# Four-head gated linear attention: own-tile products placed right behind each head's state products, gates traced later, the first two heads' sums in other PSUM banks

## The chip, the cores and the metric

The kernel runs on one core of a Trainium2 chip. The metric is the device time of one execution in microseconds (us). The engines of the core work side by side: TensorE (PE in the profile, its weight loads PEld), VectorE (DVE), ScalarE (ACT), GpSimd (POOL) and SyncE (SP, which here only starts transfers). Each engine works through its own instructions in order and waits where one needs another engine's result.

## The reference: what is computed

A trunk of two layers on 512 tokens of width 1024: layer 0 mixes with multi-head latent attention, layer 1 with gated linear attention (GLA), and each mixer is followed by a squared-ReLU MLP; a last RMS norm closes. The change touches the GLA mixer alone. Its four heads have keys of 128 and values of 256 columns. With `b_` the running sum of the log gates, the reference does per chunk of tokens:

```python
def step(state, inp):
    q_, k_, v_, b_ = inp
    o_inter = jnp.einsum('bhcd,bhde->bhce', q_ * jnp.exp(b_), state)
    ...
    attn = jnp.einsum('bhtd,bhsd,bhtsd->bhts', q_, k_, decay)
    o_intra = jnp.einsum('bhts,bhse->bhte', attn, v_)
    ...
    new_state = (state * jnp.exp(b_last[:, :, 0, :, None])
                 + jnp.einsum('bhsd,bhse->bhde', k_ * jnp.exp(b_last - b_), v_))
    return new_state, o_inter + o_intra
...
o = rms_norm(o, g_norm)
o = o * jax.nn.silu(g.astype(jnp.float32)).reshape(B, S, GLA_HEADS, GLA_HEAD_V)
return o.reshape(B, S, GLA_DV).astype(xn.dtype) @ w_o
```

The output of a head is thus a part from the tokens of its own chunk (`o_intra`) and a part from the state of all earlier chunks (`o_inter`).

## The kernel before

**Precision.** Almost every operand is held as a high part and a low part (`split`, L102: ACT writes the high part at L104, DVE the rest at L107), and a product is three matmuls, hi by hi, hi by lo and lo by hi (`mm3`, L109, lines L112 to L114). The matmuls of `apply` have a loop of their own for the three (L1335).

**Tiling of the mixer.** The kernel takes 128 tokens as a chunk, so a head has NT = 4 chunks. Heads are worked on in pairs, (0, 1) and (2, 3), by the generator `heads` (L1384):

- `gates(h)` (L1142): one matmul into a "c" bank (L1144), then ACT (L1147 and the exp and ln of L123) and DVE (L1149, L1154, L1162) turn it into the decays `B[h]` of all block sizes. Gates 0 and 1 are traced ahead of the loop, gates 2 and 3 in front of `apply` of heads 0 and 1.
- `levels(h)` (L1176): six stages that build the decayed attention within each chunk (the diagonal tiles, `at[(i, i)]`, parts ADh and ADl), the decayed queries (`at["q"]`, qd) and keys (`at["k"]`, kth and ktl). It needs `gates(h)`.
- `states(h)` (L1307): nine state matmuls (three chunks by three parts) into two "c" banks, then a chain over the chunks on ACT and DVE: each state is the sum of the chunk's product (L1317) and of the decayed former state (L1321), and is split into a high and a low part in a tile "S". There are three "S" tiles for all heads, and a head needs three.
- `apply(h)` (L1326): takes two banks ("a" for heads 0 and 2, "b" for 1 and 3; four sums of 256 columns), issues 12 matmuls of the diagonal tiles with the values (ADh and ADl in the profile), then for chunks 1 to 3 three matmuls each of the decayed queries with the state of before (S and qd in the profile). Every second chunk, ACT squares two finished sums (L1345) and DVE multiplies them by the output gate `G` (L1347), which empties the bank. Last, `small_rstd` and four multiplications by it (L1353, L1355).
- `gather(h)` (L1358): eight transposes (L129) into two "c" banks, copied out as the operands of the output projection (L1366, L1367).

**PSUM banks.** In this phase the eight banks are 2 "a", 3 "b" and 3 "c". The projections use them too: `b_type` (the values v and the output gates g, by halves of the heads) takes three "b" and an "a" (first half) or a "c" (second half), `proj_qk(1)` and `proj_qk(3)` (queries and keys of heads 2 and 3) take two "a" each. The output projection behind the mixer starts in the two "a" banks (`out_start`).

**Order.** Two generators are interleaved as the program is traced (L1415 to L1421). `proj` yields units in the order v, g, q, k, G, V: 8 units for each of v, g, G and V, and 4 for q and for k (two halves of 2 units). For each unit, the side generator `heads` is advanced by PACE = 1.27 steps:

```python
for units in main:
    pace += PACE * units
    while pace >= 1:
        next(side, None)
        pace -= 1
```

A step of `heads` ends at a `yield`: 13 for the levels of a pair, one for each `states`, five for each `apply`, one for each `gather`. It waits (a step that does nothing) until the values and output gates of its pair are there (`ready`). What is left of `heads` after the last unit runs through without a pause. The framework in which the kernel is written makes each engine's list of instructions from this trace: it follows the traced order where an instruction's buffers and operands are free by its own reckoning, and otherwise takes a later one that is ready. So the order on an engine can differ from the traced one.

Of the kernel before, what the change touches and what calls it, by code (L numbers as in the profile page):

```python
# [10 lines left out]
F32 = mybir.dt.float32  # L11
# [3 lines left out]
AF = mybir.ActivationFunctionType  # L15
ALU = mybir.AluOpType
AX = mybir.AxisListType

P = 128
D = 1024  # L20
S = 512
NT = S // P
# [12 lines left out]
HV = 256  # L35
# [15 lines left out]
def trunk_kernel(ctx: ExitStack, tc: tile.TileContext, t_in: dict, out: bass.AP, out_row: bass.AP):  # L51
    nc = tc.nc
    PE, ACT, DVE, POOL, SP = nc.tensor, nc.scalar, nc.vector, nc.gpsimd, nc.sync

    const = ctx.enter_context(tc.tile_pool(name="const", bufs=1))
    sb = ctx.enter_context(tc.tile_pool(name="sb", bufs=1))
    count = [0]

    def uname(s):
        count[0] += 1  # L60
        return f"{s}_{count[0]}"
# [14 lines left out]
    def bank(tag):  # L76
        return psum["pool"].tile([P, 512], F32, tag=f"ps_{tag}", bufs=psum["banks"][tag], name=uname("ps"))
# [144 lines left out]
    class Norm:  # L222
# [30 lines left out]
        def add(self, j, src):  # L253
            self.scaled(j, src)
            self.square(src)
# [17 lines left out]
    def small_rstd(ms, n, scale):  # L273
        l = sm(n)
        act_e(l, ms, AF.Ln, bias=eps_t, scale=scale)
        y0 = sm(n)
        act_e(y0, l, AF.Exp, scale=-0.5)
        e = sm(n)
        DVE.tensor_scalar(e, ms, scale, EPS, ALU.mult, ALU.add)
        a = sm(n)  # L280
        DVE.tensor_tensor(a, e, y0, ALU.mult)
        b = sm(n)
        DVE.scalar_tensor_tensor(b, a, -0.5, y0, ALU.mult, ALU.mult)
        r = sb.tile([P, n], F32, tag="srstd", bufs=4, name=uname("srstd"))
        DVE.scalar_tensor_tensor(r, b, 1.5, y0, ALU.add, ALU.mult)
        return r
# [721 lines left out]
    def gla(layer, nrm, vtag, ytag):  # L1008
# [34 lines left out]
        G = {}  # L1043
# [98 lines left out]
        def gates(h):  # L1142
            p = bank("c")
            PE.matmul(p, wg[:, h * P : (h + 1) * P], av, start=True, stop=True)  # L1144
            bcol = gcol("bgk", 4 * layer + h)
            l = tmp()
            ACT.activation(l, p, AF.Abs, bias=bcol)  # L1147
            m_ = tmp()
            DVE.tensor_scalar(m_, p, bcol, 0.0, ALU.add, ALU.min)  # L1149
            act_e(l, l, AF.Exp, scale=-1.0)  # L1150
            act_e(l, l, AF.Ln, bias=one_t)

            T = gp.tile([P, 2 * S], F32, tag="T", bufs=3, name=uname("T"))
            DVE.tensor_tensor(T[:, :S], m_, l, ALU.subtract)  # L1154
            n = S
            c = 0
            D_ = {}
            while n >= 4:
                D_[S // n] = T[:, c : c + n]
                if n > 4:  # L1160
                    pair_ = T[:, c : c + n].rearrange("p (n a) -> p n a", a=2)
                    DVE.tensor_tensor(T[:, c + n : c + n + n // 2], pair_[:, :, 0], pair_[:, :, 1], ALU.add)  # L1162
                c += n
                n //= 2
            act_e(T[:, :c], T[:, :c], AF.Exp, scale=GSCALE)
            B[h] = D_
# [5 lines left out]
        AT = {}  # L1172
# [131 lines left out]
        def tile_of(pair, i):  # L1304
            return cut(pair, slice(None), slice(i * P, (i + 1) * P))

        def states(h):  # L1307
            at, v = AT[h], head_values(h)
            first, last = bank("c"), bank("c")
            sums = [first[:, :HV], first[:, HV:], last[:, :HV]]  # L1310
            for i, o in enumerate(sums):
                mm3(o, tile_of(at["k"], i), v[i], True, True)
            at["S"] = []
            for i, o in enumerate(sums):
                if i:
                    s = tmp((P, HV))
                    DVE.tensor_tensor(s, o, decayed, ALU.add)  # L1317
                    o = s
                if i < NT - 2:
                    decayed = tmp((P, HV))  # L1320
                    ACT.activation(decayed, o, AF.Copy, scale=at["D"][:, i + 1 : i + 2])  # L1321
                parts = gp.tile([P, 2, HV], F32R, tag="S", bufs=3, name=uname("S"))
                split(o, parts[:, 0], parts[:, 1])
                at["S"].append((parts[:, 0], parts[:, 1]))

        def apply(h):  # L1326
            at, v = AT[h], head_values(h)
            hf = h // 2
            banks = [bank("ab"[h % 2]) for _ in range(2)]
            ms = sb.tile([P, NT], F32, tag="gms", bufs=2, name=uname("gms"))  # L1330
            os_ = [banks[i // 2][:, (i % 2) * HV : (i % 2 + 1) * HV] for i in range(NT)]

            def add(i, w, x, start, stop):
                for n, (a, b_) in enumerate(((w[0], x[0]), (w[0], x[1]), (w[1], x[0]))):
                    PE.matmul(os_[i], a, b_, start=start and n == 0, stop=stop and n == 2, skip_group_check=True)  # L1335

            for i in range(NT):
                add(i, at[(i, i)], v[i], i % 2 == 0, i == 0)
            for i in range(NT):
                if i:  # L1340
                    add(i, tile_of(at["q"], i - 1), at["S"][i - 1], False, True)
                if i % 2:
                    for r in (i - 1, i):
                        sq = tmp((P, HV))
                        ACT.activation(sq, os_[r], AF.Square, accum_out=ms[:, r : r + 1])  # L1345
                        g = G[hf][:, r, h % 2, :]
                        DVE.tensor_tensor(g, os_[r], g, ALU.mult)  # L1347
                    yield
            r = small_rstd(ms, NT, 1.0 / HV)
            for i in range(NT):  # L1350
                g = G[hf][:, i, h % 2, :]
                if i % 2:
                    ACT.activation(g, g, AF.Copy, scale=r[:, i : i + 1])  # L1353
                else:
                    DVE.tensor_scalar(g, g, r[:, i : i + 1], 0.0, ALU.mult, ALU.add)  # L1355
            yield

        def gather(h):  # L1358
            hf = h // 2
# [24 lines left out]
        def heads():  # L1384
            for h in (0, 2):
                while any(i not in qk for i in (h, h + 1, 4 + h, 5 + h)):
                    yield
                late = None
                for two in zip(levels(h), levels(h + 1)):
                    for stage in two:  # L1390
                        products = stage()
                        if late:
                            late()
                        late = products
                        yield
                late()
                yield
                while h // 2 not in ready:
                    yield
                for r in (h, h + 1):  # L1400
                    states(r)
                    yield
                for r in (h, h + 1):
                    if h == 0:
                        gates(2 + r)
                    yield from apply(r)
                for r in (h, h + 1):
                    gather(r)
                    yield
# [202 lines left out]
```

## Time and profile before

| quantity | value |
|---|---|
| three runs | 1086.86, 1087.07, 1089.51 us (median 1087.07) |
| the profiled execution | 1089.12 us |
| its span, first to last instruction | 1087.3 us |
| mean granted TensorE clock over the span | 0.998 |
| instructions | 14050 |
| L1335 (matmuls of `apply`) | 84 matmuls, started between 606.3 and 698.2 us |
| L1201 (matmuls of the attention levels) | 96, started between 552.9 and 655.9 us |
| `gla_w_in` loads | 12 of 1024 KB, 5.1 us each to landing |

In the span, the first query chunk of the mixer is read out of its bank (L1080) at 528.2 us. The first pair's `states` to `gather` lies between 598 and 637 us, between the projection of the first output gates and that of the second; the last pair's lies between 689 and 709 us, after the last unit of the projections and around the start of the output projection. Matmuls are pipelined: the profile gives a length of 0.39 us to a matmul of 512 columns whose successor starts some 0.23 us later, so the distance from start to start is what a matmul costs.

### The profile page before, as it was taken

Reading aid. Unit: us, or ns where it says so; the run is one execution under the profiler, and the core shown is the slowest. Engines: PE = TensorE matmul, PEld = TensorE weight load, DVE = VectorE, ACT = ScalarE, POOL = GpSimd, SP = SyncE. Lnnn points to the kernel's source line nnn. Section 1 sums busy time; section 2 is a strip of 40 time slices with the busy share of each in tenths; the row PEclk is TensorE's granted clock in tenths of the full one; section 3 lists DMA queues with packets and bytes.
Section 4 is the critical chain, followed back from the end, with each engine's and each line's share of the span. In section 5 each row is a group of like instructions: output and inputs, shape, how many; then the busy total and the mean of one; then the engine's idle time right before and its main releaser. Section 6 shows DMA issues by size and latency. Waiting matters only on the chain. (4 is left out here: it accounts for less than half of the span.)

```text
span 1087.3 us, 14050 instructions
## 1 busy us (share of the span) xinstructions
PE 1076.4 (99%) x5352; PEld 908.3 (84%) x5352; DVE 865.1 (80%) x1446; ACT 554.9 (51%) x947; POOL 42.1 (4%) x72
## 2 busy tenths in 40 slices
PE   9999999999999999999999999999999999999997
PEld 8888888888888888888788788888888888888886
DVE  7899968987887887887695675669798797797885
ACT  7767654553453453454446636556445444344454
POOL 8310002000000000000000000000000000000000
PEclk9999999999999999999999999999999999999999
DMA  7311232132332332322312122142233224223122
GB/s 224 88 49 39 78 116 78 61 133 78 117 116 78 116 117 78 116 78 84 93 67 88 68 78 75 42 142 68 100 115 119 78 86 133 92 80 122 71 97 78
DMA packets 86195, 101.61 MB, mean 93 GB/s; under 512 B 7440, under 2 KB 64016, under 8 KB 86128
## 3 DMA queue, kind: packets, MB, share of 16 engines
q1 hardware_dynamic: 84320, 99.67, 27.9%
q10 hardware_dynamic: 1808, 1.05, 0.3%
q8 instruction: 42, 0.69, 0.3%
q14 instruction: 25, 0.20, 0.1%
HBM read 98.35 MB, written 2.10 MB: 92 GB/s over the span
## 5 line engine op out<-in xcount | busy, mean ns | idle before, releaser
L112 PE MATMUL ps<-set,wh 128*128 128x512 f32 x760 | 297.4, 391 | 1.4 <-DVE g L1347 1.2
L113 PE MATMUL ps<-set,wh 128*128 128x512 f32 x760 | 297.1, 391 | 0.0
L114 PE MATMUL ps<-set,wl 128*128 128x512 f32 x760 | 297.0, 391 | 0.0
L104 ACT ACTIVATE wh<-wraw 128x1024 fp32r<-128x1024 f32 x139 | 147.0, 1061 | 235.0 <-PE ps L113 115.6
L107 DVE TENSOR_TENSOR wl<-wraw,wh 128x1024 fp32r<-128x1024 f32 x139 | 169.8, 1223 | 36.8 <-ACT wh L104 36.6
L112 PEld LDWEIGHTS ps<-set,wh 128*128 128x128 f32 x760 | 143.1, 188 | 31.8 <-DVE g L1347 1.8
L114 PEld LDWEIGHTS ps<-set,wl 128*128 128x128 f32 x760 | 143.1, 188 | 30.3
L113 PEld LDWEIGHTS ps<-set,wh 128*128 128x128 f32 x760 | 143.1, 188 | 27.8
L923 PE MATMUL ps<-T,wh 128*128 128x512 f32 x448 | 157.5, 391 | 0.0
L924 PE MATMUL ps<-T,wl 128*128 128x256 f32 x448 | 126.2, 282 | 0.0
L923 PE MATMUL ps<-set,wh 128*128 128x512 f32 x336 | 119.9, 397 | 0.0
L923 PEld LDWEIGHTS ps<-T,wh 128*128 128x128 f32 x448 | 84.1, 188 | 18.2
L924 PE MATMUL ps<-set,wl 128*128 128x256 f32 x336 | 94.2, 280 | 0.0
L107 DVE TENSOR_TENSOR wl<-comb,wh 128x1024 fp32r<-128x1024 f32 x42 | 51.3, 1223 | 47.0 <-ACT wh L104 46.9
L837 DVE TENSOR_TENSOR xT<-ps,xT 128x512 f32<-128x512 f32 x120 | 82.2, 685 | 7.1 <-PE ps L114 7.1
L104 ACT ACTIVATE wh<-comb 128x1024 fp32r<-128x1024 f32 x42 | 44.6, 1061 | 83.3 <-PE ps L923 81.8
L924 PEld LDWEIGHTS ps<-T,wl 128*128 128x128 f32 x448 | 84.6, 189 | 0.5
L923 PEld LDWEIGHTS ps<-set,wh 128*128 128x128 f32 x336 | 63.1, 188 | 15.1
L941 DVE TENSOR_TENSOR tmp<-ps,tmp 128x512 f32<-128x512 f32 x98 | 67.1, 685 | 0.9
L924 PEld LDWEIGHTS ps<-set,wl 128*128 128x128 f32 x336 | 63.4, 189 | 1.6
L112 PE MATMUL ps<-wh,set 128*128 128x512 f32 x144 | 58.8, 408 | 0.0
L104 ACT ACTIVATE wh<-raw 128x1024 fp32r<-128x1024 f32 x28 | 29.5, 1054 | 56.7 <-PE ps L923 55.8
(372 smaller groups left out, 1660.3 us busy)
## 6 DMA issues: line engine op xcount, KB each, us to landing
wraw<-in_mlp_w_up_dram SPq DMA_DIRECT2D x32, 1024.0 KB, 5.3
wraw<-in_mlp_w_down_dram SPq DMA_DIRECT2D x18, 1024.0 KB, 5.0
raw<-in_mlp_w_down_dram SPq DMA_DIRECT2D x14, 1024.0 KB, 4.9
wraw<-in_gla_w_in_dram SPq DMA_DIRECT2D x12, 1024.0 KB, 5.1
wraw<-in_mla_w_o_dram SPq DMA_DIRECT2D x4, 1024.0 KB, 5.2
wraw<-in_gla_w_o_dram SPq DMA_DIRECT2D x4, 1024.0 KB, 5.2
xT<-in_x_dram SPq DMA_DIRECT2D x6, 256.0 KB, 5.5
wraw<-in_mla_w_in_dram SPq DMA_DIRECT2D x3, 512.0 KB, 7.1
```

The lines of the kernel that those rows point to most:

```text
L104: order(ACT.activation(hi, src, AF.Copy))
L107: lo_eng.tensor_tensor(lo, src, f(hi), ALU.subtract)
L112: PE.matmul(psum, wh, xh, start=start, stop=False)
L113: PE.matmul(psum, wh, xl, start=False, stop=False)
L114: PE.matmul(psum, wl, xh, start=False, stop=stop)
L837: DVE.tensor_tensor(xT[m], p, xT[m], ALU.add)
L923: PE.matmul(o.rearrange("p (h t) -> p h t", h=2), wh, x, start=start and k == 0, stop=False, skip_group_check=True)
L924: PE.matmul(o[:, :TH], wl, x[:, 0], start=False, stop=k == KH - 1, skip_group_check=True)
L941: DVE.tensor_tensor(by_tile(r), high, by_tile(r), ALU.add)
```

## The change

`apply` is cut into three functions. `own_tiles(h)` takes the banks and issues the 12 matmuls of the diagonal tiles; `past(h)` issues the nine with the states, the squares and the products with the output gate; `head_norm(h)` does the rest. Each is one step of `heads`. The order for a pair becomes states(h), own_tiles(h), states(h + 1), own_tiles(h + 1), past(h), past(h + 1), head_norm(h), head_norm(h + 1), then the two gathers: ten steps where there were fourteen. Gates 2 and 3 are traced behind past(0) and past(1) instead of in front of apply(0) and apply(1). The banks of the sums are "b", "b" for head 0 and "b", "c" for head 1 ("a", "a" and "b", "b" before); heads 2 and 3 keep "a", "a" and "b", "b".

```diff
--- before.py
+++ after.py
@@ -1323,37 +1323,38 @@
                 split(o, parts[:, 0], parts[:, 1])
                 at["S"].append((parts[:, 0], parts[:, 1]))
 
-        def apply(h):
+        def add(h, i, w, x, start, stop):
+            for n, (a, b_) in enumerate(((w[0], x[0]), (w[0], x[1]), (w[1], x[0]))):
+                PE.matmul(AT[h]["o"][i], a, b_, start=start and n == 0, stop=stop and n == 2, skip_group_check=True)
+
+        def own_tiles(h):
             at, v = AT[h], head_values(h)
-            hf = h // 2
-            banks = [bank("ab"[h % 2]) for _ in range(2)]
-            ms = sb.tile([P, NT], F32, tag="gms", bufs=2, name=uname("gms"))
-            os_ = [banks[i // 2][:, (i % 2) * HV : (i % 2 + 1) * HV] for i in range(NT)]
-
-            def add(i, w, x, start, stop):
-                for n, (a, b_) in enumerate(((w[0], x[0]), (w[0], x[1]), (w[1], x[0]))):
-                    PE.matmul(os_[i], a, b_, start=start and n == 0, stop=stop and n == 2, skip_group_check=True)
-
+            banks = [bank(tag) for tag in ("bb", "bc", "aa", "bb")[h]]
+            at["o"] = [banks[i // 2][:, (i % 2) * HV : (i % 2 + 1) * HV] for i in range(NT)]
             for i in range(NT):
-                add(i, at[(i, i)], v[i], i % 2 == 0, i == 0)
+                add(h, i, at[(i, i)], v[i], i % 2 == 0, i == 0)
+
+        def past(h):
+            at, hf = AT[h], h // 2
+            at["ms"] = sb.tile([P, NT], F32, tag="gms", bufs=2, name=uname("gms"))
             for i in range(NT):
                 if i:
-                    add(i, tile_of(at["q"], i - 1), at["S"][i - 1], False, True)
+                    add(h, i, tile_of(at["q"], i - 1), at["S"][i - 1], False, True)
                 if i % 2:
                     for r in (i - 1, i):
                         sq = tmp((P, HV))
-                        ACT.activation(sq, os_[r], AF.Square, accum_out=ms[:, r : r + 1])
+                        ACT.activation(sq, at["o"][r], AF.Square, accum_out=at["ms"][:, r : r + 1])
                         g = G[hf][:, r, h % 2, :]
-                        DVE.tensor_tensor(g, os_[r], g, ALU.mult)
-                    yield
-            r = small_rstd(ms, NT, 1.0 / HV)
+                        DVE.tensor_tensor(g, at["o"][r], g, ALU.mult)
+
+        def head_norm(h):
+            r = small_rstd(AT[h]["ms"], NT, 1.0 / HV)
             for i in range(NT):
-                g = G[hf][:, i, h % 2, :]
+                g = G[h // 2][:, i, h % 2, :]
                 if i % 2:
                     ACT.activation(g, g, AF.Copy, scale=r[:, i : i + 1])
                 else:
                     DVE.tensor_scalar(g, g, r[:, i : i + 1], 0.0, ALU.mult, ALU.add)
-            yield
 
         def gather(h):
             hf = h // 2
@@ -1397,13 +1398,11 @@
                 yield
                 while h // 2 not in ready:
                     yield
-                for r in (h, h + 1):
-                    states(r)
+                for stage, r in ((states, h), (own_tiles, h), (states, h + 1), (own_tiles, h + 1), (past, h), (past, h + 1), (head_norm, h), (head_norm, h + 1)):
+                    stage(r)
+                    if stage is past and h == 0:
+                        gates(2 + r)
                     yield
-                for r in (h, h + 1):
-                    if h == 0:
-                        gates(2 + r)
-                    yield from apply(r)
                 for r in (h, h + 1):
                     gather(r)
                     yield
```

## The prediction

> **What bounds the kernel now.** I read the busy times of the page first, then the list of who waited for whom on PE, then PE's instructions in order of time around the longest of those waits, and the granted clock there.
>
> ```profile
> PE 1076.4 (99%) x5352; PEld 908.3 (84%) x5352; DVE 865.1 (80%) x1446; ACT 554.9 (51%) x947; POOL 42.1 (4%) x72
> ```
>
> PE is busy for 1076.4 of 1087.3 us, so time can only come from PE's few holes, or go into new ones. The holes of the matmul queue that were ended by an instruction of the linear attention:
>
> ```profile
> PE ps L112 <- DVE g L1347: 1.2, 1, 1.2
> PE ps L1335 <- ACT S L104: 0.6, 1, 0.6
> PE ps L1335 <- DVE S L107: 0.4, 1, 0.4
> ```
>
> The first and the third lie in the first pair of heads, the second in the last pair, the two stretches that the change edits. PE's instructions in the first (start, length, engine, line, tiles, count, then the idle time before and what ended it):
>
> ```profile
> 598.50 0.28 PE L112 MATMUL ps<-set,kth 128*128 128x256 f32 x1
> ...
> 599.56 0.40 PE L112 MATMUL ps<-set,wh 128*128 128x512 f32 x1
> ...
> 605.05 0.28 PE L112 MATMUL ps<-set,kth 128*128 128x256 f32 x1
> ...
> 606.11 0.40 PE L1144 MATMUL ps<-tmp,tmp 96*128 96x512 f32 x1
> 606.34 0.40 PE L1335 MATMUL ps<-set,ADh 128*128 128x256 f32 x2
> ...
> 607.77 1.18 PE L1335 MATMUL ps<-S,qd 128*128 128x256 f32 x9
> 608.79 0.40 PE L1335 MATMUL ps<-set,ADh 128*128 128x256 f32 x2
> ...
> 609.59 0.50 PE L1144 MATMUL ps<-tmp,tmp 96*128 96x512 f32 x1
> ...
> 610.65 1.12 PE L1335 MATMUL ps<-S,qd 128*128 128x256 f32 x7
> 612.19 0.50 PE L1335 MATMUL ps<-S,qd 128*128 128x256 f32 x2 [0.43 <-DVE S L107]
> 613.94 0.50 PE L112 MATMUL ps<-set,wh 128*128 128x512 f32 x1 [1.24 <-DVE g L1347]
> ...
> 619.09 0.39 PE L112 MATMUL ps<-set,wh 128*128 128x512 f32 x1
> ...
> 632.04 1.47 PE L129 MATMUL ps<-ident,g 128*128 128x128 f32 x12
> ```
>
> Three prices come from these rows. From 598.50 to 599.56 run nine state products of 256 columns (head 0): 1.06 us, 0.118 us each. From 599.56 to 605.05 run the 24 products of the first half of the second q chunk, 512 columns: 5.49 us. After the hole at 613.94 come the other half of q and both halves of k, 72 products, until the transposes at 632.04; those from 619.09 on, 72 - 15 = 57, take 12.95 us, 0.227 us each.
>
> The order differs from the program's. By the pacing (1.27 side steps per unit), q's second half is traced between the first and the second yield of head 0's apply; on PE it stands at 613.94, behind both heads' apply. The reason is its bank. q takes two "a" banks, apply of head 0 takes two "a" banks, and q's second half begins only when L1347 has emptied one. So PE had nothing but the two heads to run, and ran out: the nine state-times-query products of head 1 (610.65, x7, and 612.19, x2) need 9 x 0.118 = 1.06 us, but L112 starts at 613.94, 3.29 us later. **First loss: 3.29 - 1.06 = 2.23 us.**
>
> What held L1347 back is on ACT and DVE:
>
> ```profile
> 608.37 0.39 ACT L104 ACTIVATE S<-ps 128x256 fp32r<-128x256 f32 x1 [1.86 <-PE ps L1335]
> ...
> 610.36 0.67 ACT L1147 ACTIVATE tmp<-ps,gains 128x512 f32<-128x512 f32 x1
> ...
> 611.23 0.62 ACT L123 ACTIVATE tmp<-tmp 128x512 f32<-128x512 f32 x1
> 611.75 0.37 ACT L1345 ACTIVATE tmp<-ps 128x256 f32<-128x256 f32 x1
> ...
> 612.11 0.71 ACT L123 ACTIVATE tmp<-tmp,one_t 128x512 f32<-128x512 f32 x1
> ...
> 616.72 1.05 ACT L123 ACTIVATE T<-T 128x1020 f32<-128x1020 f32 x1
> ```
>
> ```profile
> 611.06 0.75 DVE L1149 TENSOR_SCALAR tmp<-ps,gains 128x512 f32<-128x512 f32 x1
> 611.73 0.41 DVE L107 TENSOR_TENSOR S<-tmp,S 128x256 fp32r<-128x256 f32 x1
> ...
> 613.47 0.42 DVE L1347 TENSOR_TENSOR g<-ps,g 128x256 f32<-128x256 f32 x1
> ```
>
> Head 1's states wait until head 0's products have read theirs (both heads share three "S" buffers): ACT's split at 608.37 follows head 0's first product, and the last lo part is written at 611.73 + 0.41 = 612.14. The gates of head 2 (L1147, L123, L1149) lie between those splits and the squares and products of head 0 (611.75, 613.47). The second L1347 ends at 613.89, and L112 starts at 613.94.
>
> Then the clock. Windows of 1 us; after the busy times of PE, PEld, DVE, ACT and POOL stands the granted clock:
>
> ```profile
> 614.00:615.00 1.00, 1.00 (x4) 0.81 (x5) 0.96 (x4) 0.42 (x3) 0.00 (x0) 0.94 0.00 0
> 615.00:616.00 1.00, 1.00 (x4) 0.75 (x3) 0.95 (x5) 1.00 (x4) 0.00 (x0) 0.50 0.00 0
> ...
> 617.00:618.00 1.00, 1.00 (x3) 0.75 (x3) 0.96 (x5) 1.00 (x2) 0.00 (x0) 0.50 0.00 0
> 618.00:619.00 1.00, 1.00 (x5) 0.83 (x4) 0.77 (x3) 1.00 (x3) 0.00 (x0) 0.85 0.00 0
> ```
>
> From 614.9 to 618.3 TensorE ran at half its clock. From 613.94 to 619.09 are 15 products, 5.15 us where 15 x 0.227 = 3.41 would do. **Second loss: 1.74 us.** Together 3.97 us, and PE is unbroken from there on to the transposes.
>
> [...]
>
> **The change part by part.**
>
> Diagonal products first. own_tiles issues the same 12 products as before (606.34 to 607.77 for head 0), right behind each head's states. They need neither S nor gates. No product, DMA or POOL instruction is added or removed, and nothing passes a queue of SP or POOL: PE's work is the same, so this edit costs 0 by itself. What it does is change cover. Counting steps at 1.27 per unit: step 20 is states of head 0, then q's first half, steps 21 and 22 own tiles of 0 and states of 1, q's second half, steps 23 to 25 own tiles of 1 and past of 0 and 1, k's first half, both norms, k's second half, both gathers. Head 0's S chain is thus covered by q. Between past(0) and past(1) no own tiles are left (they were 12 products of 0.118, 1.41 us); what is left is the gates product, 0.23 us (606.11 to 606.34).
>
> Other banks. Heads 0 and 1 now hold b, b, b, c; the "a" banks belong to q and k alone. The third "b" of the first g projection is read out at 597.34 + 0.69 = 598.03, and the next projection that needs "b" starts at 633.27:
>
> ```profile
> 597.34 0.69 ACT L1052 ACTIVATE g<-ps,rtok 128x512 f32<-128x512 f32 x1 [0.44 <-PE ps L114]
> ```
>
> ```profile
> 633.27 0.48 PE L112 MATMUL ps<-wh,set 128*128 128x512 f32 x1
> ```
>
> So q's second half has no wait, and neither 2.23 us nor the idle time that led to the slow clock has a cause: -3.97 us. The bank "c" that head 1 holds leaves two for gates, while states of head 1 hold them; I put this at 0, since its "last" bank is read out long before past(0), and k's 24 products (5.49 us) stand ready as cover. Without that cover a gates product would wait for about one split pair, 0.40 + 0.41 us (608.37 row and 611.73 row).
>
> Gates moved behind past(0) and past(1). Each gates is one product; on ACT 0.67 + 0.62 + 0.71 + 1.05 = 3.05 us, on DVE 0.75 us, a difference and seven halving adds. They leave the front of the squares and stand in front of past(1)'s splits or behind them. Their own consumer, the levels of heads 2 and 3, starts about step 30, four steps earlier than before (10 instead of 14 steps for the pair), still more than one half of k (5.49 us) after the gates. 0.
>
> Added wait. past(1) still waits for S buffers that past(0) frees. Before, that chain took from about 608.1 (three products after 607.77) to 612.14: 4.0 us. Now head 1's decays and sums can be done under q's second half, so that only the splits remain. Lower bound 0: k's products go in between, as they need no bank of the heads. Upper bound: if past(1) stands on PE directly behind, 4.0 us less the work in between (six products of past(0), one gates product, six of past(1): 0.71 + 0.23 + 0.71) = 2.4 us, with all of k queued behind it and DVE's k evacuation behind that; such a hole may also take the slow clock's 1.74 us. I take 0.4 us, by the nearest row, the 0.43 us at 612.19 in front of the same product.
>
> The last pair (heads 2 and 3; its banks stay a, a and b, b):
>
> ```profile
> 689.50 0.28 PE L112 MATMUL ps<-set,kth 128*128 128x256 f32 x1
> ...
> 692.88 0.28 PE L1335 MATMUL ps<-S,qd 128*128 128x256 f32 x1
> ...
> 695.75 0.50 PE L1335 MATMUL ps<-S,qd 128*128 128x256 f32 x3
> 696.81 1.66 PE L1335 MATMUL ps<-S,qd 128*128 128x256 f32 x6 [0.55 <-ACT S L104]
> 698.59 0.50 PE L112 MATMUL ps<-set,wh 128*128 128x512 f32 x1
> ```
>
> ```profile
> 692.51 0.42 DVE L107 TENSOR_TENSOR S<-ps,S 128x256 fp32r<-128x256 f32 x1
> ...
> 698.11 0.79 DVE L1347 TENSOR_TENSOR g<-ps,g 128x256 f32<-128x256 f32 x2 [0.21 <-ACT tmp L1345]
> ```
>
> 60 products (18 states, 24 own, 18 past) need 60 x 0.118 = 7.08 us; from 689.50 to 698.59 are 9.09, so 2.01 us are lost, at full clock:
>
> ```profile
> 689.40:699.00 9.60, 8.78 (x64) 7.75 (x63) 7.11 (x16) 6.41 (x19) 0.00 (x0) 1.00 0.17 59
> ```
>
> The end is set by ACT and DVE (states, then L1347 empties "a" at 698.5 for the output projection), which the change leaves alone. Own tiles of head 3 now come before past(2); they filled holes before and fill earlier ones now. Bounds: -2.01 (all filled) to +3.15 (past(2), at 692.88 before, is pushed back by 12 x 0.118 = 1.41 us, and the holes, now closer together, bring the slow clock, 1.74). I take 0, nearer to the first end: head 2's first S is complete at 692.51 + 0.42 = 692.93 whatever PE does before, so own tiles of head 3 that run ahead of it only use time in which PE would wait.
>
> Sum: -2.23 - 1.74 + 0.4 + 0 = -3.57 us. The profiled execution took 1089.12 us (span 1087.3 and 1.82 around it), so 1085.55 for it; the three runs shown have a median of 1087.07, 2.05 below it. Taking that difference as the profile's own, the forecast is 1087.07 - 3.57 = **1083.5**.
>
> **The rivals.**
>
> The tail gains too: own tiles ahead of past(2) free ACT and DVE to empty "a" sooner. For: 2.01 us of holes. Against: the end there is a chain of splits, not PE. 1083.5 - 2.0 = 1081.5.
>
> The slow clock is not in every run. The same instructions took 1086.86, 1087.07 and 1089.51 us, and 1089.12 with the profile: differences of 2.1 to 2.7 us, not far from the 1.74 of the slow stretch. Then the median run had none, and gains 2.23 - 0.4 only: 1085.2. Against: the holes are at the same place in every run. [...]
>
> The slow clock moves to the tail. Before, PE stood for 1.78 of 2.84 us there (695.75 to 698.59, nine products), in the first pair for 2.23 of 2.47 (its seven products end at 610.65 + 7 x 0.118 = 611.47; two more until 613.94), and only the second brought the slow clock; with own tiles spent early the holes of the tail collect. 1083.5 + 1.74 = 1085.2. [...]
>
> Slower: the S buffers. With three for two heads, past(h + 1) hangs on past(h), and the change takes away the very own tiles that lay between them. If PE's order puts past(1) before k, the hole there is 2.4 us and keeps the slow clock: 2.4 + 1.74 = 4.14 instead of 3.97; in the tail, where no k can fill, 3.15 more. 1087.07 + 0.17 + 3.15 = 1090.4. It decides from a hole of about 2 us before past(1). For: the 0.43 us wait and ACT's wait at 608.37 are this chain. Against: k is free to fill.
>
> The change does nothing for q: its second half still comes after past(1), held by something else. 1087.1.
>
> **How the numbers follow.** Forecast 0.42, tail gains 0.15, slow clock not in every run 0.10, slow clock in the tail 0.10, S buffers 0.20, no effect 0.03. 0.3% (about what a measurement of this kernel can tell from no change) is 3.26 us: below 1083.81 is faster, above 1090.33 slower. The forecast's own range, with a wait of 0 to 1.8 us, is 1083.1 to 1084.9; I count 0.31 of its 0.42 as faster. Faster 0.31 + 0.15 = 0.46; slower three quarters of the S buffers, 0.15; the same 0.39. The range runs from 1081.3, just under the filled tail, to 1089.4; above it lies most of the S buffer case, 0.17, below it 0.03.
>
> **What would show it.** Right: no wait of L112 on L1347 in the first pair; q's second half starts right behind head 1's states; granted clock 1.00 there; holes before L1335 of at most 0.6 us. Wrong: a hole of 2 us before past(1), a granted clock of 0.50 anywhere after 640, a wait for a "c" bank at the gates, or an output projection that starts later after the last V product than the 9.1 us of before.

## The result, and the profile after

| kernel | median, us | lowest to highest, us | executions | ratio to the kernel before |
|---|---|---|---|---|
| before | 1088.51 | 1086.81 to 1089.51 | 20 | |
| changed | 1086.17 | 1085.21 to 1087.95 | 20 | 0.9984 [0.9977, 0.9991] |

By the ratio, the changed kernel is faster by 0.16%, between 0.09 and 0.23%, or 1.7 us of 1088.5. The forecast was 3.57 us. The medians lie further apart (2.34 us) than the means (1088.16 and 1086.38, 1.78 us), since a varying share of each kernel's executions is some 1.5 us slower, for a reason that the experiments show. The profiled execution of the changed kernel took 1085.5 us with a span of 1083.8, so 3.5 us less span than the profiled one of before; that this is near the forecast is chance, as the experiments show.

From the page of the changed kernel, the busy times; then the whole list of who waited for whom on PE (total us, times, longest):

```profile
PE 1073.9 (99%) x5352; PEld 905.7 (84%) x5352; DVE 864.0 (80%) x1446; ACT 555.5 (51%) x947; POOL 43.4 (4%) x72
```

```profile
PE ps L1447 <- DVE ones L168: 1.2, 1, 1.2
PE ps L1328 <- ACT S L104: 0.7, 1, 0.7
PE ps L408 <- ACT set L249: 0.5, 1, 0.5
PE ps L1251 <- ACT E L1243: 0.3, 1, 0.3
PE ps L664 <- ACT pr L123: 0.2, 1, 0.2
```

The wait of the projection (L112) for the products with the gate is gone, and so is the one for DVE's S. The three-matmul helper is now L1328 (L1335 before); one wait for S of 0.7 us is left, and it is in the last pair. The first row is an old wait of the same 1.2 us under a new line number (L1448 before); it is the start of the last norm, after the mixer. The third lies at 5.5 us, at the start of the program; it isn't in the first trace of before, but is 0.7 us long in a second one. PE's instructions in the first pair (start, length, engine, line, tiles, count):

```profile
597.98 0.28 PE L112 MATMUL ps<-set,kth 128*128 128x256 f32 x1
...
599.04 0.40 PE L112 MATMUL ps<-set,wh 128*128 128x512 f32 x1
...
604.53 0.40 PE L1328 MATMUL ps<-set,ADh 128*128 128x256 f32 x2
...
605.95 0.28 PE L112 MATMUL ps<-set,kth 128*128 128x256 f32 x1
...
607.02 0.40 PE L112 MATMUL ps<-set,wh 128*128 128x512 f32 x1
...
612.48 0.40 PE L1328 MATMUL ps<-set,ADh 128*128 128x256 f32 x2
...
613.90 1.43 PE L1328 MATMUL ps<-S,qd 128*128 128x256 f32 x10
615.17 0.40 PE L112 MATMUL ps<-set,wh 128*128 128x512 f32 x1
615.41 0.51 PE L1328 MATMUL ps<-S,qd 128*128 128x256 f32 x2
...
616.68 0.36 PE L1328 MATMUL ps<-S,qd 128*128 128x256 f32 x1
...
618.38 0.40 PE L113 MATMUL ps<-set,wh 128*128 128x512 f32 x1
...
627.71 0.39 PE L112 MATMUL ps<-wh,set 128*128 128x512 f32 x1
```

Head 0's nine state products, then q's first half (599.04), head 0's own tiles (604.53), head 1's states (605.95), and right behind them q's second half (607.02), as the prediction asked for. Head 1's own tiles stand at 612.48, and from 613.90 on the 18 products of both pasts, with seven of k's products and the two gates products between them. From 613.90 to 618.38 is 4.48 us; 18 x 0.118 + 2 x 0.23 + 7 x 0.227 = 4.17 by the prediction's prices. The list of waits has no entry there, but 0.31 us are left over. As far as the rows tell, they are short waits for head 1's states: PE's row at 615.41 starts 0.05 us after DVE has written a state's low part (614.93 + 0.43), and the one at 616.68 starts 0.08 us after ACT has written the next high part (616.20 + 0.40).

```profile
614.93 0.43 DVE L107 TENSOR_TENSOR S<-ps,S 128x256 fp32r<-128x256 f32 x1 [0.16 <-ACT S L104]
```

```profile
616.20 0.40 ACT L104 ACTIVATE S<-tmp 128x256 fp32r<-128x256 f32 x1
```

Everything from the first state product to the last of k, 597.98 to 627.71, takes 29.73 us. In the first trace of before it was 598.50 to 632.04, 33.54 us.

The granted clock (the number behind the five busy times) in two of the windows where it was 0.50 before:

```profile
615.00:616.00 1.00, 1.00 (x8) 0.80 (x7) 0.69 (x2) 0.22 (x1) 0.00 (x0) 1.00 0.00 0
...
617.00:618.00 1.00, 1.00 (x8) 0.87 (x7) 0.79 (x4) 0.82 (x4) 0.00 (x0) 1.00 0.00 0
```

In the last pair:

```profile
685.33 0.28 PE L112 MATMUL ps<-set,kth 128*128 128x256 f32 x1
...
690.45 2.01 PE L1328 MATMUL ps<-S,qd 128*128 128x256 f32 x12
693.13 1.65 PE L1328 MATMUL ps<-S,qd 128*128 128x256 f32 x6 [0.67 <-ACT S L104]
694.92 0.50 PE L112 MATMUL ps<-set,wh 128*128 128x512 f32 x1
```

From the pair's first state product to the output projection 694.92 - 685.33 = 9.59 us, 0.50 more than before (9.09). All own tiles of head 3 now stand ahead of past(2): its first product starts 690.45 - 685.33 = 5.12 us after the pair's first state product, where it was 692.88 - 689.50 = 3.38 us before. Behind it the 18 products of both pasts take 694.92 - 690.45 = 4.47 us for 18 x 0.118 = 2.12 us of work. So 2.35 us of idle time are gathered in one place. ACT shows the price: its split of head 3's first state, in the trace of before and of the changed kernel.

```profile
694.69 0.37 ACT L104 ACTIVATE S<-ps 128x256 fp32r<-128x256 f32 x1
```

```profile
691.06 0.39 ACT L104 ACTIVATE S<-ps 128x256 fp32r<-128x256 f32 x1 [0.45 <-PE ps L1328]
```

Before, it starts 694.69 - 689.50 = 5.19 us after the pair's first state product; now 691.06 - 685.33 = 5.73, and ACT waited 0.45 us for PE, because the "S" tile that it writes is free only when past(2) has read it. 0.54 us later there, 0.50 us later at the output projection.

For the experiments, three distances are read in every trace: from head 0's first state product to head 2's (first pair, the second projection of g and its like); from there to the first product of the output projection; from head 2's first state product to the end of the span.

| profiled execution | states 0 to states 2 | states 2 to output projection | states 2 to end | half clock |
|---|---|---|---|---|
| before | 91.00 | 9.09 | 397.80 | at 614.9 to 618.3 |
| before, unchanged, again | 89.41 | 9.09 | 397.78 | none |
| changed | 87.35 | 9.59 | 398.47 | none |
| changed, again | 87.37 | 9.58 | 399.98 | in the tail |
| changed, third | 87.34 | 9.59 | 400.02 | in the tail |
| banks only | 87.03 | 9.08 | 397.78 | none |
| order only | 89.08 | 9.59 | 398.43 | none |
| changed, last pair's banks too | 87.34 | 6.58 | 396.66 | none |
| changed, fourth S tile | 86.72 | 9.15 | 399.57 | in the tail |
| changed, gates in front | 87.11 | 9.57 | 398.45 | none |
| old order, banks of both pairs | 87.06 | 6.60 | 396.61 | none |
| the same, fourth S tile | 87.22 | 6.61 | 396.68 | none |

The last column speaks of the two edited stretches. Two executions of one program agree within 0.1 us in these distances where the clock is the same, so differences of 0.3 us can be read.

### The profile page after: what moved, and what is told of

It is laid out like the page before. It is cut to its first block, busy times and chain, and to the rows that moved or that the text cites. A ratio compares the mean times of both kernels' runs of the same rounds, so it can differ in the third digit from the quotient of the medians.

```text
span 1083.8 us, 14050 instructions
## 1 busy us (share of the span) xinstructions
PE 1073.9 (99%) x5352; PEld 905.7 (84%) x5352; DVE 864.0 (80%) x1446; ACT 555.5 (51%) x947; POOL 43.4 (4%) x72
## 4 chain that ended last, share of the span: by engine, by line
PE 97%; DVE 1%; ACT 1%; DMA 0%; issue 0%; SPq 0%; DVEq 0%; ACTq 0%
PE ps L112 21%; PE ps L114 21%; PE ps L113 21%; PE ps L923 17%; PE ps L924 9%; PE ps L1201 2%; PE ps L129 1%; PE ps L408 1%; PE ps L871 1%; PE ps L1328 1%; PE ps L671 0%; PE ps L667 0%; PE ps L670 0%; PE ps L1251 0%; PE ps L669 0%; DMA gains<-in_gains_dram 0%
## 5 line engine op out<-in xcount | busy, mean ns | idle before, releaser
L112 PE MATMUL ps<-set,wh 128*128 128x512 f32 x760 | 296.8, 391 | 0.1
L112 PEld LDWEIGHTS ps<-set,wh 128*128 128x128 f32 x760 | 142.7, 188 | 30.2 <-DVE g L1348 0.3
L112 PE MATMUL ps<-wh,set 128*128 128x512 f32 x144 | 58.4, 406 | 0.0
```

The source lines that it names most:

```text
L112: PE.matmul(psum, wh, xh, start=start, stop=False)
```

## The experiments

**Is the half clock in every execution of before?** The kernel before, unchanged, once more.

> The kernel before, unchanged, profiled a second time. In its first profile the first pair (from head 0's first state product to the last of q's and k's products) took 33.54 us, with 2.23 us of holes and 1.74 us of slow clock. Theory A (the slow clock follows from the holes in every execution): granted clock 0.50 for some 3.4 us behind the hole again, 33.5 us. Rival B (the slow clock comes in some executions only): holes of about 2.2 us, granted clock 1.00, about 31.8 us. Ratio of the times 1.000 in both.

Measured: 1088.63 us over 11 executions (1086.93 to 1089.52), ratio 1.0005 [0.9997, 1.0014]. Its profiled execution took 1086.93 us. PE and the clock in that one:

```profile
610.03 1.13 PE L1335 MATMUL ps<-S,qd 128*128 128x256 f32 x7
611.60 0.51 PE L1335 MATMUL ps<-S,qd 128*128 128x256 f32 x2 [0.43 <-DVE S L107]
613.34 0.50 PE L112 MATMUL ps<-set,wh 128*128 128x512 f32 x1 [1.24 <-DVE g L1347]
```

```profile
614.00:615.00 1.00, 1.00 (x6) 0.83 (x5) 0.93 (x5) 1.00 (x4) 0.00 (x0) 1.00 0.00 0
615.00:616.00 1.00, 1.00 (x6) 0.81 (x6) 0.98 (x5) 1.00 (x6) 0.00 (x0) 1.00 0.00 0
```

The same two holes, 0.43 and 1.24 us, in the same places, and full clock behind them: 89.41 us where the first profile had 91.00, 1.6 us less. So the half clock is not a consequence of these holes in every execution. Of 54 executions of the kernel before whose mean granted clock is known, 24 had 0.999 and took 1086.59 to 1088.12 us; 30 had 0.998 or less and took 1088.18 to 1089.56. The two groups do not overlap, and their means lie 1.6 us apart (1087.36 and 1088.93). That the dip sits behind the first pair in all 30 is argued from the two profiles, not shown.

**The banks without the order.** The kernel before with the changed kernel's banks:

```diff
-            banks = [bank("ab"[h % 2]) for _ in range(2)]
+            banks = [bank(tag) for tag in ("bb", "bc", "aa", "bb")[h]]
```

> The kernel before with only the banks of the sums changed (b, b for head 0, b, c for head 1), old order. Theory (the banks carry the gain): no wait of L112 on L1347 in the first pair, which takes 29.5 to 30 us; the last pair stays at 9.1 us; ratio to before 0.998 or lower, and about 0.5 us faster than the changed kernel, whose last pair took 9.59 us. Rival (the own tiles in front are needed as cover too): a hole of 1 to 2 us before head 1's state-times-query products, the first pair at 31 us or more, ratio 0.999 to 1.000.

Measured: 1084.7 us (1084.3 to 1085.36, 8 executions), ratio 0.9971 [0.996, 0.9981]. In the first pair:

```profile
608.05 0.51 PE L1335 MATMUL ps<-S,qd 128*128 128x256 f32 x3
608.40 0.39 PE L112 MATMUL ps<-set,wh 128*128 128x512 f32 x1
...
613.89 0.87 PE L1335 MATMUL ps<-S,qd 128*128 128x256 f32 x6
```

In the old order of stages, head 0's own tiles and its first three products with a state run, then q's second half from 608.40 on with no wait, then the other six of head 0 at 613.89. The list of waits has no entry of L112 for the gate products. From states 0 to states 2 are 87.03 us, 2.38 less than in the profile of before without the half clock, and the last pair keeps its 9.08 us. The banks alone do all of what the change does in the first pair. The eight executions lie at 1085.36 us or below and the changed kernel's twenty at 1085.21 or above, so this kernel seems to be the faster one, though the two intervals of the ratio still touch (0.9981 and 0.9977).

**The order without the banks.** The changed kernel with the old banks:

```diff
-            banks = [bank(tag) for tag in ("bb", "bc", "aa", "bb")[h]]
+            banks = [bank(tag) for tag in ("aa", "bb", "aa", "bb")[h]]
```

> The changed kernel with the old banks (a, a and b, b for the first pair), new order and gates moved. Theory (the banks carry the gain): q's second half still waits for an a bank behind head 1's products, the first pair takes 32 us or more (a hole of 2 us or more), the last pair 9.6 us; ratio to before 1.000 to 1.002. Rival (the order carries the gain): the first pair at 30 us, ratio 0.998.

Measured: 1087.41 us (1087.03 to 1090.42, 11 executions), ratio 0.9999 [0.999, 1.0008]: no difference.

```profile
608.45 1.23 PE L1328 MATMUL ps<-S,qd 128*128 128x256 f32 x9
...
611.20 1.65 PE L1328 MATMUL ps<-S,qd 128*128 128x256 f32 x6 [0.41 <-ACT S L104]
613.04 0.50 PE L112 MATMUL ps<-set,wh 128*128 128x512 f32 x1 [0.19 <-DVE g L1348]
```

q's second half is again behind both heads' products with the states, at 613.04, and again released by the gate product (L1348 in this file). From 608.45 to 613.04 are 4.59 us, for 18 x 0.118 + 2 x 0.23 = 2.58 us of work: 2.0 us of holes, only in smaller pieces than before; to the last of k the pair takes 31.61 us, where 32 or more was expected. The order brings 0.33 us in the first pair (89.08 against 89.41) and costs 0.50 in the last (9.59).

**The last pair's banks.** The same move of banks for heads 2 and 3, on top of the change:

```diff
-            banks = [bank(tag) for tag in ("bb", "bc", "aa", "bb")[h]]
+            banks = [bank(tag) for tag in ("bb", "bc", "bb", "bc")[h]]
```

> The changed kernel with the last pair's sums in b, b and b, c too, so that the output projection's two a banks are free when it starts. Theory (the 2.5 us lost in the last pair are a bank wait like the first pair's): output projection products fill the holes; from head 2's first state product to the end of its first 24 products and head 3's last state-times-query product no hole over 0.5 us; 2 us less than the changed kernel, ratio to before 0.996 to 0.9975. Rival (the end there is the chain of states on ACT and DVE, and the transposes behind it wait as much later): the holes move behind the 24 products, in front of the gather transposes, and the time is that of the changed kernel, 0.998.

Measured: 1084.13 us (1083.47 to 1084.21, 5 executions), ratio 0.9966 [0.9953, 0.9978].

```profile
685.74 0.28 PE L112 MATMUL ps<-set,kth 128*128 128x256 f32 x1
...
692.32 0.39 PE L112 MATMUL ps<-set,wh 128*128 128x512 f32 x1
...
693.24 0.28 PE L1328 MATMUL ps<-S,qd 128*128 128x256 f32 x1
...
694.41 0.40 PE L1328 MATMUL ps<-S,qd 128*128 128x256 f32 x2
```

The output projection now starts at 692.32, 6.58 us after the pair's first state product at 685.74, and past(3)'s last products go in between its own. What held it in the last pair was thus the same as in the first: an "a" bank that L1347 empties. Of the 3.0 us that it starts earlier, the span keeps 398.47 - 396.66 = 1.8. Of the other 1.2, 6 x 0.118 = 0.7 are those last six products, which now run behind its start, and the list of waits has a new entry, for the transposed outputs:

```profile
PE ps L112 <- ACT set L1367: 0.3, 1, 0.3
```

**Is the tail's 0.50 us the S tiles?** One more tile for states, used by the first state of heads 1 and 3, so that past(h) need not have read its own first:

```diff
-                parts = gp.tile([P, 2, HV], F32R, tag="S", bufs=3, name=uname("S"))
+                if h % 2 and i == 0:
+                    parts = gp.tile([P, 2, HV], F32R, tag="E", bufs=1, name=uname("S"))
+                else:
+                    parts = gp.tile([P, 2, HV], F32R, tag="S", bufs=3, name=uname("S"))
```

> The changed kernel, but the first state part of heads 1 and 3 goes into the buffer of tag E, which is free then, so that it needn't wait for past(0) or past(2) to release an S buffer. Theory (the last pair grew from 9.09 to 9.59 us because head 2's first state-times-query product now stands behind head 3's own tiles, so that the S buffer comes free later and head 3's chain starts later): ACT's split of head 3's first state starts 0.5 us or more earlier than in the changed kernel (5.73 us after head 2's first state product there), the last pair takes 9.1 us or less, and the time is 0.4 to 0.6 us below the changed kernel. Rival (ACT and DVE are full in that stretch and set its end): 9.5 us or more as before.

Measured: 1085.0 us (1084.29 to 1088.49, 7 executions), ratio 0.9969 [0.9958, 0.9981]. ACT's split of head 3's first state, and PE around it:

```profile
692.31 0.37 ACT L104 ACTIVATE S<-ps 128x256 fp32r<-128x256 f32 x1
```

```profile
687.13 0.28 PE L112 MATMUL ps<-set,kth 128*128 128x256 f32 x1
...
692.23 1.57 PE L1331 MATMUL ps<-S,qd 128*128 128x256 f32 x12
694.49 1.66 PE L1331 MATMUL ps<-S,qd 128*128 128x256 f32 x6 [0.69 <-ACT S L104]
696.28 0.50 PE L112 MATMUL ps<-set,wh 128*128 128x512 f32 x1
```

692.31 - 687.13 = 5.18 us, as before the change (5.19) and without the wait for PE; the output projection stands at 696.28 - 687.13 = 9.15 us. So the wait for the tile made 0.44 of the 0.50; the 9.1 us expected are missed by 0.05. The first pair gains too, 87.35 to 86.72, which was not expected and fits the short waits for states there. By its ratio the kernel can't be told from the changed one, as the intervals overlap. The profiled execution is the slowest of the seven (1088.49 us): it had the half clock in the tail, and its first state product stands at 600.41 us, some 2 us later than in the other traces, for a reason before the edited stretches that stays open.

**The changed kernel again, twice.** For the spread of its own executions, 1085.21 to 1087.95.

> The changed kernel, unchanged, profiled a second time. Theory (its spread of 1085.2 to 1087.9 us comes from the slow clock in the last pair, in a third of the executions): either all windows from 590 to 720 at granted clock 1.00 and a time of about 1085.7, or 0.50 for some 3.4 us behind head 3's state-times-query products and a time of 1086.7 or more. Rival (the spread has to do with something else, such as the loads at the start): granted clock 1.00 between 20 and 1075 us whatever the time.

> The changed kernel, unchanged, profiled a third time, with the expectations of the second: granted clock 0.50 behind head 3's state-times-query products if the time is 1086.7 or more, 1.00 if it is 1086.5 or less; the rival expects 1.00 between 20 and 1075 us at any time.

Measured: 1087.29 and 1087.15 us, one execution each, both profiled. In both the first pair is as in the first profile (87.37 and 87.34), and both have the half clock behind the tail's holes. Windows of the first of them:

```profile
695.00:696.00 1.00, 0.87 (x3) 0.71 (x3) 0.51 (x2) 0.51 (x4) 0.00 (x0) 0.53 0.00 0
696.00:697.00 1.00, 1.00 (x3) 0.79 (x3) 0.87 (x3) 0.90 (x6) 0.00 (x0) 0.50 0.00 0
697.00:698.00 1.00, 1.00 (x4) 0.74 (x3) 0.91 (x5) 1.00 (x5) 0.00 (x0) 0.50 0.00 0
698.00:699.00 1.00, 1.00 (x5) 0.82 (x4) 0.85 (x4) 0.97 (x5) 0.00 (x0) 0.76 0.00 0
```

The tail takes 399.98 and 400.02 us where it took 398.47: 1.5 us. Of the changed kernel's 20 executions, seven took 1086.67 us or more and thirteen 1085.21 to 1086.54; the profile without the dip (1085.5) lies in the second group, these two (1087.29, 1087.15) within the span of the first. That the other executions of that group have the dip in the tail too is argued from this, and the two groups are only 0.13 us apart.

**Gates back in front.** The changed kernel with gates 2 and 3 traced in front of past(0) and past(1):

```diff
-                    stage(r)
                     if stage is past and h == 0:
                         gates(2 + r)
+                    stage(r)
```

> The changed kernel with gates 2 and 3 traced in front of past(0) and past(1), as the kernel before had them in front of apply. Theory (moving the gates costs and brings nothing, since q's and k's products cover both places): from head 0's first state product to the second g projection 29.7 us, to head 2's first state product 57.6 us, the last pair 9.6 us, each within 0.2 us of the changed kernel, no hole over 0.5 us in the first pair. Rival (the gates in front of the squares and products delay the banks and head 1's states, as in the kernel before): holes of 0.5 us or more before head 1's state-times-query products, the first stretch at 30.3 us or more.

Measured: 1086.1 us, one execution. 87.11 against 87.35 us from states 0 to states 2, 9.57 against 9.59 behind. The 0.24 us is just above the 0.2 that the expectation allowed; no hole over 0.5 us appears in the first pair. The place of the gates decides nothing that one execution shows.

**The best of it.** The kernel before, in its old order, with the banks of both pairs moved:

```diff
-            banks = [bank("ab"[h % 2]) for _ in range(2)]
+            banks = [bank(tag) for tag in ("bb", "bc", "bb", "bc")[h]]
```

> The kernel before with only the banks changed, in both pairs (b, b and b, c). Theory (the banks are the whole gain and the new order costs): first pair as in the run with only the first pair's banks (30.71 us to the second g projection), output projection's first product at most 7 us after head 2's first state product, no granted clock under 1.00 before 1070 us; ratio to before 0.996 to 0.997, and not slower than the kernel with the new order and both pairs' banks (0.9966). Rival (the new order helps once the banks are free): 0.5 us or more slower than that kernel.

Measured: 1083.63 us (1082.96 to 1083.99, 5 executions), ratio 0.9957 [0.9944, 0.9969]. The last pair:

```profile
685.69 0.28 PE L112 MATMUL ps<-set,kth 128*128 128x256 f32 x1
...
691.94 0.52 PE L1335 MATMUL ps<-S,qd 128*128 128x256 f32 x3
692.29 0.39 PE L112 MATMUL ps<-set,wh 128*128 128x512 f32 x1
...
693.21 0.28 PE L1335 MATMUL ps<-S,qd 128*128 128x256 f32 x1
...
694.38 0.40 PE L1335 MATMUL ps<-S,qd 128*128 128x256 f32 x2
```

6.60 us from states 2 (685.69) to the output projection (692.29), head 3's last six products with the states spread through it, and the executions lie within 1.0 us of each other. One line gives 4.7 us (0.43% of 1088.5), against 1.7 of the change; the expectation had said 0.3 to 0.4%. The version with the new order and the same banks (0.9966) isn't told apart from it, as the intervals overlap.

**The fourth tile on top of that.** The edit of the fourth state tile on the kernel just shown.

> The kernel before with both pairs' banks in b, b and b, c and a fourth state buffer (tag E) for the first state of heads 1 and 3. Theory (with the output projection as cover, head 3's chain no longer sets PE's end, so an earlier chain brings nothing): last pair at 6.6 us to the output projection, 396.6 us from head 2's first state product to the end of the span, ratio to before 0.995 to 0.9965, the same as without the fourth buffer. Rival (the S buffers still hold up the transposes behind the output projection): 0.3 us or more less from head 2's first state product to the end.

Measured: 1083.59 us (1083.22 to 1083.91, 4 executions), ratio 0.9953 [0.9937, 0.997]; 87.22 and 6.61 us in the two stretches. No difference: where the output projection filled PE, an earlier state gained nothing (396.68 against 396.61 us to the end).

## Why the prediction was right in direction and twice too large

**First loss, 2.23 us, and the 0.4 of the added wait: right.** Against the kernel before without the half clock, the first stretch went from 89.41 to 87.35 us: -2.06, where -2.23 + 0.4 = -1.83 was predicted. The cause is as predicted, the "a" bank (banks only: -2.38; order only: -0.33). The term of 0.4 held too: there is no hole of 2 us before past(1), as k's products do go in between, and the 0.31 us left over there are, as far as the rows tell, short waits for head 1's states. With the banks moved, the new order costs 87.35 - 87.03 = 0.32 us in this pair.

**Second loss, 1.74 us: the step that failed.** It was real in the one profile shown and stood in the sum as if in every execution; then it was taken off a median in which, by its time, it was not. The step is "Taking that difference as the profile's own": 1089.12 against 1087.07 was no property of profiling, most of it was the half clock of that execution. The term is also 0.12 us too large, since the same 15 products take 616.87 - 613.34 = 3.53 us at full clock in the second profile, not 3.41: the half clock cost 5.15 - 3.53 = 1.62. At 1.57 us, the distance of the two groups, in 30 of 54 executions it is worth some 0.87 us on average. The objection to the rival, "the holes are at the same place in every run", is refuted by the second profile of before: same holes, full clock (the last section has what differed). The rival's 1085.2 us is close to the changed kernel's profiled 1085.5, which had no half clock in the two edited stretches either.

**The tail, 0: wrong by 0.5 to 0.7 us.** "Own tiles of head 3 that run ahead of it only use time in which PE would wait" fails here. PE had other work in that time: before, its first long wait in the last pair stood 696.81 - 689.50 = 7.3 us behind the first state product, and past(2) ran from 3.38 us on. The step looked at head 2's states alone. Past(2) also frees the S tiles for head 3's states, and it now starts 1.74 us later after states 2 (5.12 against 3.38). The S-buffer rival named just this chain, with 1.41 us of own tiles in front; the end moved by 0.50 us, since ACT came to its split only 0.45 us before the tile was free, and only that part of the delay was left. The prediction's own sign for it, an output projection later than 9.1 us, is there, and the one S wait left is 0.67 us where at most 0.6 was allowed. Another 0.19 us lies behind the start of the output projection ((398.47 - 9.59) - (397.78 - 9.09)), which goes with the new order (order only: 398.43 - 9.59 = 388.84 against 388.69). Nearly all of it lies in head 3's eight transposes, which take 703.09 - 702.09 = 1.00 us, and 704.42 - 703.60 = 0.82 in the second trace of before; the fourth of them starts at 702.57, just after ACT's last multiplication by the norm ends (701.61 + 0.91 = 702.52). The rival's other half, a hole before past(1) in the first pair, did not come.

**The half clock in the tail: a rival at 0.10 that holds in part.** The mechanism was as put there: own tiles spent early, holes collected (2.35 us in 4.47). Its price is 1.5 us, not 1.74, in about a third of the executions (7 of 20 by their times), so some 0.5 us on average. The sign "a granted clock of 0.50 anywhere after 640" says nothing by itself: every trace, before's too, has it behind the last matmul (from 1085.92 us on in the first trace of before, whose last matmul starts at 1080.56; from 1079.84 on in the first of the changed kernel, whose last starts at 1077.03), where no product is left to slow.

The sum by what was measured: -2.06 (first pair) + 0.50 + 0.19 (tail) - 0.87 (half clock gone in front) + 0.53 (half clock come behind) = -1.71 us, or 0.16%, as the comparison of executions has it. Against the forecast of -3.57, the half clock in front makes 0.87 us of the shortfall, the tail 0.69 and the half clock behind 0.53; the first pair gave 0.23 more. The profile-to-profile difference of 3.5 us is another sum: 91.00 - 87.35 = 3.65 with the half clock in full, less 398.47 - 397.80 = 0.67 in the tail, and 598.50 - 597.98 = 0.52 from before the first state product, which the change doesn't touch.

**What was put at 0.** These were the own tiles by themselves, the "c" bank and the place of the gates. (The price of 0.40 us for ACT's split there is 0.39 in its row; nothing rests on it.) Own tiles were not tried apart from the rest of the order; in the last pair it is they that push past(2) back. The gates bear it out by their own experiment (0.24 us and less). The "c" bank shows no wait in the list of the changed kernel nor in that of the kernel with banks only.

**The chances.** The range held the time. Faster by over 0.3% had the largest chance, and the gain of 0.16% lies in the case between; the rival of the half clock that is not in every run was right, and deserved more than 0.10, as three times of 1086.86, 1087.07 and 1089.51 us with a profile of 1089.12 already were two groups 2 us apart.

## What to carry to other kernels

Before a term from one profile is taken off a median, see whether that profile belongs to the same group of executions as the median: a spread as large as the term itself says that it may not. A slow stretch that only some executions have is worth its price times its share. When a stage waits for a bank, move the bank first and by itself: here one line gave more than the reordering around it. When filler work is moved ahead, look at what the work that it delays sets free, not only at what that work waits for.

## What the runs showed of the hardware

The half clock followed the same holes in some executions and not in others. The kernel before, with 0.43 and 1.24 us of holes (2.23 of 2.47 us idle in all), slowed down behind them in one profile and not in the other, and by the mean clock in about 30 of 54 executions. The changed tail, whose longest single wait is 0.67 us (2.35 of 4.47 us idle), did so in two of three profiles. It took about 3.4 us in both places: 614.9 to 618.3 before, and in the tail's four windows shown above 3.42 us (a window of 1 us with clock c was at half for 2 x (1 - c): 0.94 + 1 + 1 + 0.48).

What differs can be read from the traces. In each of the twelve, every change of the granted clock lies a whole number of 3.413 us behind the first one (in the first trace of before at 7.31, 614.88, 618.30 and 1085.92 us, which is 0, 178, 179 and 316 times 3.413 later), and the first one differs, from 4.33 to 10.82 us. So the changes lie on a grid of windows of 3.413 us, whose place is another one in each execution. Count as idle what a matmul's distance to the next exceeds the median for its shape. Then the 16 such windows at full clock that the half clock follows hold 2.02 us of idle time or more, and the other 3760 hold 1.89 or less. In the first profile of before, 2.33 us of the first pair's idle time fell into one window (611.47 to 614.89); in the second, a border at 611.90 split the same holes into 1.00 and 1.53. In the changed tail, a border at 694.14 split them in the first profile, and in the next the window from 691.65 to 695.07 held 2.22 us. If all places of the windows are equally likely, one would take in 1.9 to 2.0 us in a share of 0.44 to 0.51 of the executions of before and 0.37 to 0.48 of the changed kernel's, an estimate from these traces; 30 of 54 and 7 of 20 were counted. With the banks of both pairs moved, no place of a window takes in 1.0 us in the edited stretches, and those executions lie within 1.0 us of each other.
